# A two-layer hybrid attention block: biases added in PSUM by a two-row product, evictions moved to ScalarE, one minimum taken by a reduction

## The chip, the core and the metric

The kernel runs on one core of one Trainium2 chip. The metric is the device time of one execution in microseconds; of several runs the median counts. TensorE (PE), VectorE (DVE), ScalarE (ACT), GpSimd (POOL) and SyncE (SP) each work through their own queue of instructions in order. Transfers are issued from the queues of SP and ACT.

## What is computed

The reference is a two-layer block over 2048 latent tokens and 256 context tokens of width 1024. Cut to what matters here:

```python
h = rmsnorm(x, norm_g) * (1.0 + scale) + shift          # and the same for ctx
p = split_proj(h @ w_in + b_in)                         # one projection, 18 parts, 4368 columns
ya = diff_attention(...)   # 4 heads x 2 softmax maps, every query over 2304 keys
yb = hgrn2_mixer(...)      # gated linear recurrence, both directions
yc = window_gqa(...)       # windowed attention with sinks
yd = mlstm_mixer(...)      # both directions; output times sigmoid(og)
mixed = concatenate([ya, yb, yc, yd]) * silu(p[18])
x = x + gate * (mixed @ w_out)

def attend(qs, ks, vs):                                 # differential attention
    s = einsum('mbhqd,mbhkd->mbhqk', qs, ks) * scale    # m = 0, 1: the two maps
    p = softmax(s, axis=-1)
    w = p[0] - lam * p[1]
    return einsum('bhqk,bhkv->bhqv', w, vs)
```

The bias `b_in` of the projection, and the shift that each softmax row gets before its exponential, are what the change touches.

## The kernel before

Each of the two layers goes through the same stages. First the rows are normalised and transposed (`hps`, `ht`), and split into two half-precision parts `hh` and `hl`. The weights are scaled by 256 (`WS`) and split the same way by `load_w`. A product of the projection is then three matmuls in 16 bits for each of 8 chunks of the inner dimension.

The projection has two forms. `proj_fm` gives column blocks with the features on the partitions; their bias is a column and comes in with ACT's eviction. `proj_tm` ("token-major") gives 128 tokens on the partitions; here the bias runs along the free dimension. For these `bias_row` loads the bias broadcast over all 128 partitions into a tile `bg` with two buffers, and DVE evicts the PSUM tile `ptm` by one `scalar_tensor_tensor` (`stt`, line 111: times 1/256, plus `bg`). Nine weight blocks of a layer are token-major: VA, MV, HI, SV, OG and four GATE blocks. The tiles that take evictions come from two tags that rotate: `tmp` (six buffers) and `tmp2` (tag `t2`, three buffers).

After the first blocks (VA, KA, QA) runs the loop over differential attention. It has 72 units (a head and 128 queries) in layer 0 and 64 in layer 1. In each unit and for each map `m` (1 first, then 0), `diff_scores` computes the scores in two PSUM tiles, `sc0` of 1024 columns and `sc1` of 1280, one buffer each, and DVE takes the minimum of each (line 1048). The smaller of the two minima is the row's shift (line 1054 for map 1, an operation of the helper `tt` at line 108; line 1056 for map 0). `diff_exp` exponentiates both tiles on ACT. The next map's scores need the PSUM tiles free, that is, after those exponentials. `diff_mix` combines the maps of the unit before on DVE (line 111, `p<-p,sm,p`), ACT rounds the result, and POOL computes the rest of the rounding (`p<-p,p`, line 108).

The other weight blocks of the layer (`other_blocks`) are a "filler": a heavy and a light list of blocks, whose matmuls `pump` lays between those of attention. How much is pumped is fixed in `pe_ns`, an account of TensorE time that `mm` keeps at 2.4 GHz: `FSTEP` between the two score tiles and `FGAP` after each map. A block whose weights were just requested waits `WLOAD` (22,000 to 32,192 ns of that account) before it goes on. In this loop TensorE's order is that of the code; the other engines' order comes from a scheduler, which also brings a transfer forward as soon as its tile has a free buffer. What is left of the filler after the last unit runs in `rest_stream`, beside the start of windowed attention and mLSTM. The last stage of a layer weaves windowed attention, mLSTM, HGRN2 and the output projection (`fx`).

Of the kernel before, what the change touches and what calls it, by code (L numbers as in the profile page):

```python
# [10 lines left out]
F32 = mybir.dt.float32  # L11
# [35 lines left out]
IWS = 1.0 / WS  # L47
GROUPS = [(0, 512), (512, 512), (1024, 512), (1536, 512), (2048, 256)]
# [25 lines left out]
def kernel(  # L74
# [44 lines left out]
    SP.dma_start(ident, masks[:, 0:P])  # L119

# [138 lines left out]
    for l in range(n_layers):  # L259
# [252 lines left out]
        def proj_tm(w, ts, n):  # L512

            yield True
            ps = pps.tile([P, 512], F32, tag="pp", name="ptm")
            for i, t in enumerate(ts):
                g, o = t // 4, (t % 4) * P
                d = ps[:, i * n:(i + 1) * n]
                for k in range(KC):
                    h_, l_ = hh[g][:, k, o:o + P], hl[g][:, k, o:o + P]  # L520
                    mm(d, h_, w[:, 0, k], k == 0, False)
                    mm(d, h_, w[:, 1, k], False, False)
                    mm(d, l_, w[:, 0, k], False, k == KC - 1)
                    yield
            return ps[:, :len(ts) * n].rearrange("p (t c) -> p t c", c=n)
# [68 lines left out]
        def bias_row(c0, n):  # L594

            bg = stg.tile([P, 272], F32, tag="bg", name="bg", bufs=2)[:, :n]
            SP.dma_start(bg, b_in[l, c0:c0 + n].partition_broadcast(P))
            return bg

        def tm_out(w, ts, bg, n):  # L600
            ps = yield from proj_tm(w, ts, n)
            s = tmp2("tm")[:, :len(ts) * n].rearrange("p (t c) -> p t c", c=n)
            stt(s, ps, IWS, bc(bg, 1, len(ts)), ALU.mult, ALU.add)
            return s
# [8 lines left out]
        def proj_store_tm(w, c0, dst, need=True):  # L613
            bg = bias_row(c0, 256)
            for ts in tile_sets(2, need):
                s = yield from tm_out(w, ts, bg, 256)
                DQ.dma_start(rows_of(dst, ts), s)

        def proj_split_tm(w, n, c0, dst):
            nh = n // 64  # L620
            bg = bias_row(c0, n)
            for ts in tile_sets(2):
                s = (yield from tm_out(w, ts, bg, n)).rearrange("p t (h d) -> p t h d", d=64)
                s16 = stg.tile([P, 2, 4, P], F16, tag="sp", name="s16", bufs=2)
                sv = s16[:, :len(ts), :nh]
                A.copy(sv[:, :, :, 0:64], s)
                tt(G, sv[:, :, :, 64:128], s, sv[:, :, :, 0:64], ALU.subtract)
                for i, t in enumerate(ts):
                    DQ.dma_start(dst[t * P:(t + 1) * P], sv[:, i])

        def mix_values(w, gates):

            bg = bias_row(C_MV, 272)
            for t in all_tiles():
                ps = (yield from proj_tm(w, [t], 272))[:, 0]
                s = tmp("tm")
                stt(s[:, :272], ps, IWS, bg, ALU.mult, ALU.add)
                V.tensor_copy(gates[:, t], s[:, 256:272])
                DQ.dma_start(dmv[t * P:(t + 1) * P], s[:, :256])
# [270 lines left out]
        def gate_silu(w, cb):  # L910
            bg = bias_row(C_GATE + cb * 256, 256)
            for ts in tile_sets(2, cq):
                ps = yield from proj_tm(w, ts, 256)
                z, a_ = tmp2("gz"), tmp2("ga")
                stt(z.rearrange("p (t c) -> p t c", c=256), ps, IWS, bc(bg, 1, 2), ALU.mult, ALU.add)
                V.tensor_scalar(z, z, ZLOW, None, ALU.max)
# [31 lines left out]
        def other_blocks():  # L948
# [4 lines left out]
            def values(w):  # L953
# [16 lines left out]
                ((C_OG, 256), lambda w: proj_store_tm(w, C_OG, dog, cq)),  # L970
# [57 lines left out]
        with ExitStack() as st2:  # L1028
# [7 lines left out]
            def diff_scores(u, m):  # L1036
# [16 lines left out]
                if m:  # L1053
                    u["nm"] = tt(V, sm[:, 5:6], sm[:, o:o + 1], sm[:, o2:o2 + 1], ALU.min)
# [146 lines left out]
        with ExitStack() as st4:  # L1201
# [166 lines left out]
            def mlstm_load(i):  # L1368
# [25 lines left out]
                V.tensor_scalar(og, og, ZLOW, None, ALU.max)  # L1394
# [339 lines left out]
```

## Time and profile before

| | us |
|---|---|
| median of 3 runs | 4094.21 |
| lowest and highest | 4089.32 to 4104.06 |
| the profiled execution, whole | 4102.18 |
| its span, first to last instruction | 4100.4 |

The span leaves 1.8 us of the profiled execution outside. That execution is 8.0 us above the median. TensorE's mean granted clock was 0.913 of its full speed. Busy time of an engine is the time in which it had an instruction under way; idle time is put down to what ended it.

### The profile page before, as it was taken

Reading aid. Unit: us, or ns where it says so; the run is one execution under the profiler, and the core shown is the slowest. Engines: PE = TensorE matmul, PEld = TensorE weight load, DVE = VectorE, ACT = ScalarE, POOL = GpSimd, SP = SyncE. Lnnn points to the kernel's source line nnn. Section 1 sums busy time; section 2 is a strip of 40 time slices with the busy share of each in tenths; the row PEclk is TensorE's granted clock in tenths of the full one; section 3 lists DMA queues with packets and bytes.
Section 4 is the critical chain, followed back from the end, with each engine's and each line's share of the span. In section 5 each row is a group of like instructions: output and inputs, shape, how many; then the busy total and the mean of one; then the engine's idle time right before and its main releaser. Section 6 shows DMA issues by size and latency. Waiting matters only on the chain. (4 is left out here: it accounts for less than half of the span.)

```text
span 4100.4 us, 77666 instructions
## 1 busy us (share of the span) xinstructions
PE 3358.2 (82%) x29798; PEld 2269.8 (55%) x29798; DVE 2831.4 (69%) x4343; ACT 2330.9 (57%) x4662; POOL 2375.0 (58%) x1701
## 2 busy tenths in 40 slices
PE   6988878888768996888888988778887698758888
PEld 4656645444546765555557466444445476545554
DVE  5158888888896647465544398988888865467665
ACT  4245655556655636566654266656666665456764
POOL 4443455443445538798966535665334564488885
PEclk8999989999989995898889999999998899869999
DMA  6356866667656628577845457667676584366783
GB/s 211 91 149 150 186 136 159 140 141 154 145 128 157 161 95 200 149 194 185 205 119 177 126 125 151 135 140 155 148 162 142 125 193 116 106 162 170 183 194 104
DMA packets 1267259, 622.12 MB, mean 152 GB/s; under 512 B 931972, under 2 KB 1214152, under 8 KB 1266888
## 3 DMA queue, kind: packets, MB, share of 16 engines
q1 hardware_dynamic: 1164520, 490.65, 53.1%
q10 hardware_dynamic: 102368, 126.52, 9.2%
q8 instruction: 234, 3.83, 0.4%
q14 instruction: 137, 1.12, 0.1%
HBM read 291.76 MB, written 131.23 MB: 103 GB/s over the span
## 5 line engine op out<-in xcount | busy, mean ns | idle before, releaser
L108 POOL TENSOR_TENSOR p<-p,p 128x1024 f16<-128x1024 f32 (+2 forms) x264 | 629.4, 2385 | 792.7 <-ACT p L1084 722.8
L105 ACT ACTIVATE p<-scr,sm 128x1024 f32<-128x1024 f32 (+2 forms) x528 | 628.3, 1194 | 417.8 <-DVE sm L1073 145.2
L94 PE MATMUL ptm<-wb,hh 128*128 128x256 f16 (+2 forms) x5024 | 835.6, 273 | 32.6 <-DVE dSs L111 7.9
L1048 DVE TENSOR_REDUCE sm<-scr 128x1 f32<-128x1024 f32 (+2 forms) x528 | 699.3, 1327 | 218.3 <-PE scr L94 214.5
L94 PE MATMUL pfm<-hh,wb 128*128 128x512 f16 (+1 forms) x2592 | 805.7, 375 | 32.7 <-DVE gz L111 10.1
L94 PE MATMUL ptm<-wb,hl 128*128 128x256 f16 (+2 forms) x2512 | 672.1, 273 | 1.7 <-POOL hl L108 1.7
L94 PEld LDWEIGHTS <-wb 128*128 128x128 f16 x3888 | 378.1, 101 | 414.3 <-issue 84.0
L94 PE MATMUL scr<-Ks,Qs 128*128 128x512 f16 (+1 forms) x1296 | 364.8, 381 | 284.5 <-ACT p L105 279.4
L94 PEld LDWEIGHTS <-hh 128*128 128x128 f16 x5024 | 480.1, 100 | 133.9 <-issue 40.0
L94 PE MATMUL pfm<-hl,wb 128*128 128x512 f16 (+1 forms) x1296 | 485.6, 375 | 0.0
L111 DVE SCALAR_TENSOR_TENSOR p<-p,sm,p 128x1024 f32<-128x1024 f32 (+2 forms) x264 | 413.8, 1568 | 8.1
L94 PEld LDWEIGHTS <-Qs 128*128 128x128 f16 x1296 | 130.7, 102 | 425.2 <-issue 354.5
L94 PE MATMUL fx<-wo,mh 128*128 128x512 f16 x1088 | 342.4, 396 | 16.8 <-DVE xt L111 8.5
L1084 ACT CAST p<-p 128x1024 f16<-128x1024 f32 (+2 forms) x264 | 297.7, 1128 | 39.2 <-DVE p L111 33.8
L94 PEld LDWEIGHTS <-wt 128*128 128x128 f16 x4640 | 243.9, 102 | 71.4 <-DMA wt<-p 24.4
L94 PE MATMUL pv<-Vs,wt 128*128 128x128 f16 (+1 forms) x4640 | 258.5, 213 | 21.9 <-DMA wt<-p 13.5
L94 PEld LDWEIGHTS <-hl 128*128 128x128 f16 x2512 | 250.8, 100 | 35.4 <-POOL hl L108 3.4
L108 POOL TENSOR_TENSOR ph<-swp,ph 128x640 f16<-128x640 f32 (+2 forms) x136 | 196.0, 1442 | 53.7 <-ACT ph L1335 44.3
L108 POOL TENSOR_TENSOR E<-lk,cm 128x512 f32<-128x512 f32 (+1 forms) x136 | 204.8, 1506 | 34.6 <-DMA cm<-dhc 17.8
L94 PE MATMUL fx<-wo,mlo 128*128 128x512 f16 x544 | 212.9, 391 | 1.4 <-DVE mlo L108 1.1
L105 ACT ACTIVATE E<-E 128x1024 f32<-128x1024 f32 x136 | 143.2, 1054 | 102.8 <-POOL E L108 98.9
L108 DVE TENSOR_TENSOR QQ<-hq,E 128x512 f32<-128x512 f32 x119 | 143.8, 1214 | 65.2 <-ACT E L105 46.7
(301 smaller groups left out, 6577.2 us busy)
## 6 DMA issues: line engine op xcount, KB each, us to landing
wraw<-in_w_in_dram SPq DMA_DIRECT2D x60, 512.0 KB
dgt<-ga ACTq DMA_DIRECT2D x68, 256.0 KB
r1b<-dr SPq DMA_DIRECT2D x68, 256.0 KB
gtt<-dgt SPq DMA_DIRECT2D x34, 512.0 KB
mraw<-in_w_mod_dram SPq DMA_DIRECT2D x64, 256.0 KB
vi<-dhi SPq DMA_DIRECT2D x49, 256.0 KB
KSb<-dsk SPq DMA_DIRECT2D x56, 192.0 KB
Ks<-dka SPq DMA_DIRECT2D x64, 144.0 KB
```

What stands on the lines that cost most here:

```text
L94: PE.matmul(o, lhsT=lhsT, rhs=rhs, start=start, stop=stop)
L105: A.activation(out=o, in_=i, func=f, **kw)
L108: return e.tensor_tensor(out=o, in0=a, in1=b, op=op)
L111: V.scalar_tensor_tensor(out=o, in0=a, scalar=s, in1=b, op0=op0, op1=op1)
L1048: V.tensor_reduce(sm[:, m * 2 + j:m * 2 + j + 1], ps[:, :n], AX.X, ALU.min)
L1084: A.copy(wl[:, :n], p[:, :n])
```

## The change

A constant tile `bones` of 2 x 128 elements, all 16.0, is made once. `bias_row` now loads the bias to two partitions only, into a buffer of the tag `t2`, and makes from it a two-row half-precision tile by five small DVE instructions: scale, round, subtract, mask, combine. Row 0 is the rounded bias, row 1 the rest. In `proj_tm` each tile's accumulation in PSUM begins with a product of `bones` with these two rows, so that the bias is in PSUM. The evictions of HI and MV become ACT copies, the two halves of VA and SV come straight from PSUM (ACT the rounded one, DVE the rest, where POOL computed it before), and the evictions of OG and GATE become one DVE `tensor_scalar` that also applies the floor `ZLOW`. The two instructions that applied that floor before (lines 916 and 1394) are gone. Map 1's shift is taken by one `tensor_reduce` over the two minima, in place of a `tensor_tensor` of the two.

```diff
@@ -45,6 +45,7 @@
 EPS = 1e-6
 WS = 256.0
 IWS = 1.0 / WS
+BONES = 16.0
 GROUPS = [(0, 512), (512, 512), (1024, 512), (1536, 512), (2048, 256)]
 C_QA, C_KA, C_VA = 0, 256, 512
 C_HQ, C_FF, C_FB, C_HI = 768, 1024, 1280, 1536
@@ -117,6 +118,8 @@
     V.memset(eps_t, EPS)
     V.memset(one_t, 1.0)
     SP.dma_start(ident, masks[:, 0:P])
+    bones = const.tile([2, P], F16, tag="bones", name="bones")
+    V.memset(bones, BONES)
 
     def rstd_of(o, ss, n):
 
@@ -509,16 +512,17 @@
                 yield
             return ps
 
-        def proj_tm(w, ts, n):
+        def proj_tm(w, ts, n, bg):
 
             yield True
             ps = pps.tile([P, 512], F32, tag="pp", name="ptm")
             for i, t in enumerate(ts):
                 g, o = t // 4, (t % 4) * P
                 d = ps[:, i * n:(i + 1) * n]
+                mm(d, bones, bg, True, False)
                 for k in range(KC):
                     h_, l_ = hh[g][:, k, o:o + P], hl[g][:, k, o:o + P]
-                    mm(d, h_, w[:, 0, k], k == 0, False)
+                    mm(d, h_, w[:, 0, k], False, False)
                     mm(d, h_, w[:, 1, k], False, False)
                     mm(d, l_, w[:, 0, k], False, k == KC - 1)
                     yield
@@ -593,14 +597,23 @@
 
         def bias_row(c0, n):
 
-            bg = stg.tile([P, 272], F32, tag="bg", name="bg", bufs=2)[:, :n]
-            SP.dma_start(bg, b_in[l, c0:c0 + n].partition_broadcast(P))
+            bf = tmp2("bg")[0:2, :n]
+            SP.dma_start(bf, b_in[l, c0:c0 + n].partition_broadcast(2))
+            hv, bg = [stg.tile([2, 272], F16, tag=f"bg{j}", name="bg16", bufs=1 + j)[:, :n] for j in range(2)]
+            V.tensor_scalar(bf, bf, WS / BONES, None, ALU.mult)
+            V.tensor_copy(hv, bf)
+            tt(V, bf, bf, hv, ALU.subtract)
+            V.tensor_scalar(bf, bf, ident[0:2, 1:2], None, ALU.mult)
+            stt(bg, hv, ident[0:2, 0:1], bf, ALU.mult, ALU.add)
             return bg
 
-        def tm_out(w, ts, bg, n):
-            ps = yield from proj_tm(w, ts, n)
+        def tm_out(w, ts, bg, n, low=False):
+            ps = yield from proj_tm(w, ts, n, bg)
             s = tmp2("tm")[:, :len(ts) * n].rearrange("p (t c) -> p t c", c=n)
-            stt(s, ps, IWS, bc(bg, 1, len(ts)), ALU.mult, ALU.add)
+            if low:
+                V.tensor_scalar(s, ps, IWS, ZLOW, ALU.mult, ALU.max)
+            else:
+                act(s, ps, AF.Copy, scale=IWS)
             return s
 
         def tile_sets(per, need=True):
@@ -610,21 +623,22 @@
         def rows_of(dst, ts):
             return dst[ts[0] * P:(ts[0] + len(ts)) * P].rearrange("(t p) ... -> p t ...", p=P)
 
-        def proj_store_tm(w, c0, dst, need=True):
+        def proj_store_tm(w, c0, dst, need=True, low=False):
             bg = bias_row(c0, 256)
             for ts in tile_sets(2, need):
-                s = yield from tm_out(w, ts, bg, 256)
+                s = yield from tm_out(w, ts, bg, 256, low)
                 DQ.dma_start(rows_of(dst, ts), s)
 
         def proj_split_tm(w, n, c0, dst):
             nh = n // 64
             bg = bias_row(c0, n)
             for ts in tile_sets(2):
-                s = (yield from tm_out(w, ts, bg, n)).rearrange("p t (h d) -> p t h d", d=64)
-                s16 = stg.tile([P, 2, 4, P], F16, tag="sp", name="s16", bufs=2)
-                sv = s16[:, :len(ts), :nh]
-                A.copy(sv[:, :, :, 0:64], s)
-                tt(G, sv[:, :, :, 64:128], s, sv[:, :, :, 0:64], ALU.subtract)
+                s = (yield from proj_tm(w, ts, n, bg)).rearrange("p t (h d) -> p (t h) d", d=64)
+                s16 = stg.tile([P, 2, 512], F16, tag="sp", name="s16", bufs=2).rearrange("p a (h d) -> p (a h) d", d=P)
+                s16 = s16[:, :len(ts) * nh]
+                act(s16[:, :, 0:64], s, AF.Copy, scale=IWS)
+                stt(s16[:, :, 64:128], s, IWS, s16[:, :, 0:64], ALU.mult, ALU.subtract)
+                sv = s16.rearrange("p (t h) d -> p t h d", h=nh)
                 for i, t in enumerate(ts):
                     DQ.dma_start(dst[t * P:(t + 1) * P], sv[:, i])
 
@@ -632,10 +646,10 @@
 
             bg = bias_row(C_MV, 272)
             for t in all_tiles():
-                ps = (yield from proj_tm(w, [t], 272))[:, 0]
+                ps = (yield from proj_tm(w, [t], 272, bg))[:, 0]
                 s = tmp("tm")
-                stt(s[:, :272], ps, IWS, bg, ALU.mult, ALU.add)
-                V.tensor_copy(gates[:, t], s[:, 256:272])
+                act(s[:, :256], ps[:, 0:256], AF.Copy, scale=IWS)
+                act(gates[:, t], ps[:, 256:272], AF.Copy, scale=IWS)
                 DQ.dma_start(dmv[t * P:(t + 1) * P], s[:, :256])
 
         carry = stg.tile([P, 2, 65], F32, tag="carry", name=f"carry{l}")
@@ -910,10 +924,9 @@
         def gate_silu(w, cb):
             bg = bias_row(C_GATE + cb * 256, 256)
             for ts in tile_sets(2, cq):
-                ps = yield from proj_tm(w, ts, 256)
+                ps = yield from proj_tm(w, ts, 256, bg)
                 z, a_ = tmp2("gz"), tmp2("ga")
-                stt(z.rearrange("p (t c) -> p t c", c=256), ps, IWS, bc(bg, 1, 2), ALU.mult, ALU.add)
-                V.tensor_scalar(z, z, ZLOW, None, ALU.max)
+                V.tensor_scalar(z.rearrange("p (t c) -> p t c", c=256), ps, IWS, ZLOW, ALU.mult, ALU.max)
                 sigmoid(a_, z)
                 tt(G, a_, a_, z, ALU.mult)
                 DQ.dma_start(rows_of(dgt, ts)[:, :, cb * 256:(cb + 1) * 256], a_.rearrange("p (t c) -> p t c", c=256))
@@ -967,7 +980,7 @@
             light = [
                 ((C_HI, 256), lambda w: proj_store_tm(w, C_HI, dhi)),
                 ((C_SV, 128), lambda w: proj_split_tm(w, 128, C_SV, dsv)),
-                ((C_OG, 256), lambda w: proj_store_tm(w, C_OG, dog, cq)),
+                ((C_OG, 256), lambda w: proj_store_tm(w, C_OG, dog, cq, True)),
                 ((C_MQ, 256), lambda w: proj_store_fm(w, 13, 1.0, dmq, cq)),
                 ((C_HQ, 256), lambda w: proj_store_fm(w, 7, 0.125, dhq, cq)),
             ] + [((C_GATE + cb * 256, 256), lambda w, cb=cb: gate_silu(w, cb)) for cb in range(4)]
@@ -1051,7 +1064,7 @@
                 o2 = o + len(hs) - 1
 
                 if m:
-                    u["nm"] = tt(V, sm[:, 5:6], sm[:, o:o + 1], sm[:, o2:o2 + 1], ALU.min)
+                    u["nm"] = V.tensor_reduce(sm[:, 5:6], sm[:, o:o2 + 1], AX.X, ALU.min)
                 else:
                     u["nm"] = V.tensor_scalar(sm[:, 4:5], sm[:, o:o + 1], sm[:, o2:o2 + 1], shf, ALU.min, ALU.add)
 
@@ -1391,7 +1404,6 @@
                     tt(G, r1b[:, d], r1b[:, d], bc(mlm[:, d], 1, 4), ALU.add)
                     for h in range(4):
                         act(r1b[:, d, h], r1b[:, d, h], AF.Exp, bias=TM[:, 0, d, js[d] * 4 + h:js[d] * 4 + h + 1])
-                V.tensor_scalar(og, og, ZLOW, None, ALU.max)
                 sigmoid(og, og)
                 return js, qt_, kt_, v1, r1b, g0b, og
 
```

## Rows read from the trace of the kernel before

**Rows 1.** Windows: length, busy us of PE, PEld, DVE, ACT, POOL, clock, DMA, GB/s.
```profile
300.00:1350.00 1050.00, 850.03 (x7440) 569.11 (x7433) 855.78 (x1277) 616.36 (x1054) 487.24 (x297) 0.93 0.67 150
1350.00:1450.00 100.00, 92.74 (x809) 70.78 (x808) 60.12 (x116) 55.04 (x125) 52.67 (x47) 0.98 0.59 149
1450.00:1580.00 130.00, 112.07 (x974) 84.26 (x972) 70.06 (x120) 60.59 (x116) 67.59 (x57) 0.85 0.46 128
1580.00:2115.00 535.00, 439.23 (x4598) 306.44 (x4601) 313.56 (x549) 336.24 (x895) 460.11 (x363) 0.84 0.72 179
...
2370.00:3255.00 885.00, 703.46 (x6217) 460.75 (x6215) 786.64 (x1099) 560.94 (x874) 433.73 (x236) 0.94 0.67 144
```

**Rows 2.** Waits in layer 0's attention loop, 300 to 1350 us.
```profile
PE scr L94 <- ACT p L105: 117.2, 81, 7.1
```

**Rows 3.** Waits in layer 1's attention loop, 2400 to 3330 us.
```profile
PE scr L94 <- ACT p L105: 141.8, 103, 6.3
```

**Rows 4.** Instructions on tile sm (ns min/median/max, first and last start).
```profile
L108 DVE TENSOR_TENSOR sm<-sm x136: 127/772/2330, 247.9 to 3240.4; 128x1 f32<-128x1 f32 x136
L1056 DVE TENSOR_SCALAR sm<-sm,shf x136: 244/272/277, 257.2 to 3248.0; 128x1 f32<-128x1 f32 x136
L1073 DVE TENSOR_REDUCE sm<-sm x136: 136/144/158, 263.0 to 3252.4; 128x2 f32<-128x4 f32 x128, 128x2 f32<-128x2 f32 x8
```

**Rows 5.** Timeline of one unit, 2808 to 2814 us (start, us, instruction, idle before).
```profile
2808.90 2.61 POOL L108 TENSOR_TENSOR p<-p,p 128x1280 f16<-128x1280 f32 x1 [3.35 <-ACT p L1084]
...
2810.41 1.12 DVE L108 TENSOR_TENSOR sm<-sm 128x1 f32<-128x1 f32 x1
...
2811.62 1.11 ACT L105 ACTIVATE p<-scr,sm 128x1024 f32<-128x1024 f32 x1 [1.65 <-DVE sm L1073]
...
2812.20 1.28 DVE L111 SCALAR_TENSOR_TENSOR p<-p,sm,p 128x1024 f32<-128x1024 f32 x1
...
2812.88 0.59 PE L94 MATMUL scr<-Ks,Qs 128*128 128x512 f16 x2 [0.67 <-ACT p L105]
...
2813.51 1.23 DVE L1048 TENSOR_REDUCE sm<-scr 128x1 f32<-128x1024 f32 x1
```

**Rows 6.** Groups by line and shape (busy us, mean ns, idle before).
```profile
L108 DVE TENSOR_TENSOR sm<-sm 128x1 f32<-128x1 f32 x136 | 97.8, 719 | 0.6
...
L916 DVE TENSOR_SCALAR gz<-gz 128x512 f32<-128x512 f32 x68 | 47.4, 697 | 1.4
...
L722 ACT COPY kT<-ktp 128x512 f32<-128x512 f32 x32 | 18.5, 578 | 20.8 <-PE ktp L101 14.5 <-POOL ga L108 3.6 <-DVE gz L111 2.4
...
L111 DVE SCALAR_TENSOR_TENSOR tm<-ptm,bg 128x272 f32<-128x272 f32 x36 | 15.6, 432 | 2.0 <-PE ptm L94 2.0
L638 DVE COPY gates<-tm 128x16 f32<-128x16 f32 x36 | 15.2, 421 | 0.2
...
L163 ACT COPY mrow<-modps 128x256 f32<-128x256 f32 x32 | 11.9, 372 | 14.5 <-PE modps L94 14.4
```

**Rows 7.** Instructions on tile gz, whole run.
```profile
L111 DVE SCALAR_TENSOR_TENSOR gz<-ptm,bg x68: 659/683/693, 1067.4 to 3568.0; 128x512 f32<-128x512 f32 x68
L916 DVE TENSOR_SCALAR gz<-gz x68: 395/460/2197, 1069.2 to 3569.1; 128x512 f32<-128x512 f32 x68
```

**Rows 8.** The last of the 136 pairs, minimum and scores behind it (timeline).
```profile
3240.41 0.15 DVE L108 TENSOR_TENSOR sm<-sm 128x1 f32<-128x1 f32 x1
...
3241.84 1.01 PE L94 MATMUL scr<-Ks,Qs 128*128 128x512 f16 x2 [4.45 <-ACT p L105]
```

**Rows 9.** Timeline of block VA: three token-major products in a row.
```profile
111.04 0.38 PE L94 MATMUL ptm<-wb,hh 128*128 128x256 f16 x2
...
111.37 0.38 PE L94 MATMUL ptm<-wb,hh 128*128 128x256 f16 x2
```

**Rows 10.** Timeline: a bias row's transfer, and the first eviction that uses it.
```profile
495.02 0.53 SPq L597 DMA_DIRECT2D bg<-in_b_in_dram  x1
...
1067.45 0.68 DVE L111 SCALAR_TENSOR_TENSOR gz<-ptm,bg 128x512 f32<-128x512 f32 x1
```

## The prediction

> **What bounds the kernel now.** I read first the busy times by stretch. No stretch is idle and no engine is the bound of all of them. The two loops over attention take 1050 and 885 us, nearly half of the span; there DVE is busy for 82% and 89%, TensorE for 81% and 79% [rows 1]. Behind the first loop, where the rest of the filler runs, TensorE is busy for 93% and then 86%: it sets the pace. In the last stage of layer 0 POOL is busy for 460 of 535 us [rows 1].
>
> Next the waits inside the loops. TensorE's wait before a score tile, ended by ACT's exponential, sums to 117 us in layer 0 and 142 us in layer 1, together 259 us [rows 2, 3]. That is most of TensorE's idle time there (200 and 182 us by [rows 1]). So a cycle sets the pace of the loop: scores, the two minima on DVE, the smaller of them, exponential on ACT, next scores. The filler is laid into it by an account and fills the gaps only partly. Whoever shortens the cycle shortens the loop, until the 259 us are used up.
>
> Then the small instruction that takes the smaller minimum. Map 1's is a `tensor_tensor` of one element per partition; it takes 127 ns at least, 772 ns at the median and 2330 ns at most. Its neighbours of the same size hardly vary: 244 to 277 ns for map 0's `tensor_scalar`, 136 to 158 ns for a two-element `tensor_reduce` [rows 4]. The timeline of one unit says why: POOL's subtraction runs from 2808.90 to 2811.51, the minimum begins at 2810.41 and ends at 2811.53, with POOL [rows 5]. I compared all 136 minima with POOL's instructions, the first at 247.9 and the last at 3240.4 [rows 4]: of the 83 that took over 0.2 us, 82 end within 0.06 us of the end of a POOL instruction. DVE waits for POOL inside the instruction. The exponential, and then the next scores, wait behind it.
>
> **The change part by part.**
>
> *Map 1's minimum.* Removed: 136 times 719 ns, 97.8 us [rows 6]. Added: 136 reductions of two elements, 0.146 us each by the nearest row [rows 4]: 20 us. DVE gets back 78 us. What of it reaches the end of the loop depends on whether TensorE waited behind that minimum. I took each minimum and the wait of the scores behind it; the last pair is 0.15 us and 4.45 us [rows 8]. Summing the smaller of "duration less 0.14" and "wait" over the 136 pairs gives 57 us. A second limit is DVE's own order: after the minimum come three small instructions and the mix of the two maps (`p<-p,sm,p`), and the next minimum of scores follows directly, at 2813.51 after 2812.20 plus 1.28 [rows 5]. The mix has two tensor inputs too and may still wait for POOL. Then only the 0.67 us from the end of the minimum (2811.53) to the mix (2812.20), which now pass while POOL works, and about 0.1 us of the minimum itself are won. With a cap of 0.75 us per unit the sum over the pairs is 45 us. I take 48; bounds 15 (a third of the capped sum) and 57.
>
> *DVE's other relief in the loop.* HI's 18 evictions at 0.683 us [rows 7] are 12 us, MV's 36 evictions and 36 copies of gates are 15.6 and 15.2 us [rows 6], all moved to ACT. The 68 floors of GATE at 0.697 us are 47 us [rows 6]; by their starts 25 of them (the first at 1069.2 [rows 7]) fall into the loops, some 17 us. Together about 60 us of DVE time in a cycle in which DVE is busy for 82 to 89%. The minimum's own relief, 78 us, gave 45 to 57 us by the pairs, over half; here instructions stand anywhere in the cycle, so I take a third: 22 us, bounds 8 and 35. OG's and GATE's evictions stay on DVE at about the 0.68 us that they take. VA and SV keep one instruction each on DVE and on ACT, and POOL is freed of 36 subtractions, which I count as nothing: POOL is busy for less than half of the loops.
>
> *Outside the loops.* Some 40 floors of GATE and 34 of OG go, the latter on half as many columns, together some 50 us of DVE time, where TensorE or POOL sets the pace [rows 1]. I take 5 us, bounds 0 and 15.
>
> *ACT's new evictions.* HI: 18 at 0.578 us, by the PSUM copy of the same shape; MV: 36 at 0.372 and 36 of 16 columns at about 0.2 (an estimate, by the two fixed parts of those two rows: 0.578 less twice the 0.206 for 256 columns leaves 0.17) [rows 6]. That is 10 + 13 + 7 = 30 us on an engine that is busy for 59 to 63% of the loops and belongs to the cycle. I take a sixth on the path: 5 us, bounds 0 and 20.
>
> *The two-row products.* There are 162 tiles in layer 0 and 152 in layer 1 (five blocks leave out the two context tiles), 314 products. A row of two partitions is not in the trace; nearest are products of 256 columns over all rows: from 111.04 to 111.37 three begin, 0.11 us each [rows 9]. I price the new ones alike, since what streams is the same columns; SV's 36 have half. That is 278 x 0.11 + 36 x 0.055 = 33 us at full clock. In the loops the filler is metered by the account, which counts these products, so each unit takes the same TensorE time and the surplus moves behind the loop, where TensorE sets the pace. I take nine tenths of it as lost: 30 us, bounds 25 and 36 (33 divided by the mean clock of 0.913).
>
> *The bias rows.* 18 blocks, five DVE instructions each on up to 272 columns: 90. Nearest are 0.16 us at least (it must exceed a two-element reduction's 0.146 [rows 4]) and the 0.46 us median of the floor on 512 columns [rows 7]. Seven blocks get their bias inside the loops; 35 instructions at 0.33 are 12 us of DVE, of which I count 5 on the path, bounds 3 and 20. The floor's maximum of 2197 ns beside its median of 460 shows that this kind of instruction can be held up as the minimum was [rows 7]. The Trainium skill ("SBUF — State Buffer", "SBUF: two separate sides") says that GpSimd and VectorE share a port pair which the first one holds for a whole instruction, against VectorE instructions with two SBUF inputs or in a two-port mode; 82 of the 83 slow minima agree. By that rule most of the five can be held up like the floor, at its mean of 0.697 us: 63 us of DVE in all instead of 30, and 9 or 10 us on the path instead of 5. I stay with 5, because they can run long before they are needed; the upper bound covers the rest.
>
> *The wait for the bias.* It was needed at a block's first eviction and is now needed at its first product, with all of TensorE's queue behind it, in the loop the next unit's scores too. Before, the transfer ran up to 572 us ahead (495.02, first used at 1067.45 [rows 10]). Now it needs one of the three buffers of `t2`, which the evictions of the block before rotate through. But a block waits 22 to 32 us for its weights, so those are done by then. I count nothing; the rival below has the price.
>
> **Sum.** -48 - 22 - 5 + 5 + 30 + 5 = -35 us. The profiled execution took 4102.2, its span 4100.4 with 1.8 us around it, so it would take 4067. It lay 8 us above the median of the runs shown; the prediction of the median is 4094 - 35, rounded to 4060.
>
> **The rivals.**
>
> *More is won.* Pairs without the cap (57), the other relief in full (35), 15 outside, and small costs (0 + 25 + 3): -79, 4015. For it speaks that 259 us of waits are there to be used up [rows 2, 3]; against it that DVE stays close to full.
>
> *The wait moves on.* The minimum no longer waits for POOL, but the mix behind it does, and the next minimum of scores is behind the mix on DVE. If the reach is a third (15), other relief 8, nothing outside, costs as above (+40): +17, 4111. The rule of the skill named above would have it so, for the mix has two SBUF inputs. Against it: what stands between, 0.67 us, runs under POOL's time, and ACT starts earlier in any case [rows 5].
>
> *Slower: blocks wait for their bias.* Place: the first product of each of 18 blocks. Price: a transfer, then five dependent instructions in DVE's queue between those of a unit that fills DVE for over 80%. At 5 us a block it is 90 us, 4150; from 35 / 18 = 1.9 us a block on the gain is gone. For it speaks that the tile comes from a busy tag; against it the long lead of the transfer before [rows 10].
>
> **How the numbers follow.** Forecast (4035 to 4080) 0.55; more won 0.18; the wait moves on 0.13; blocks wait 0.10; something else, such as an unlucky order by the scheduler, 0.04. Under 0.3%, 12 us, a measurement of this kernel can't tell a difference from none (its three runs span 15 us). Faster: 0.55 + 0.18 and a little of the others, 0.75. Of the wait that moves on about half lies within 12 us, with part of the others: 0.11 the same, 0.14 slower. The range takes in more won (with 10 us below it) and ends at the wait that moves on: 4005 to 4112; beyond lies the slower rival.
>
> **What would show it.** Right: map 1's new reduction takes about 0.15 us with no spread, and the waits of scores for the exponential fall well below 259 us while both loops end earlier, together by some 65 us. The loops' gain should be partly given back behind them, about 15 us a layer. The mix's mean time on DVE may rise. Wrong: first products of a block that wait for DVE's bias tile; loops as long as before, with the same waits named after the mix or after ACT's evictions; or two-row products that take much more than 0.11 us.

## The result: 1.5% slower, and the profile after

| | median of runs (us) | lowest to highest | profiled run, its span | mean granted clock |
|---|---|---|---|---|
| before | 4094.26 (4) | 4089.32 to 4104.06 | 4102.2, 4100.4 | 0.913 |
| changed | 4155.61 (4) | 4139.32 to 4171.28 | 4171.28, 4169.2 | 0.910 |

The ratio of the medians is 1.015, its 95% interval 1.010 to 1.019. The forecast was 4060 in 4005 to 4112: the changed kernel lies 44 us above the upper end, on the other side of the kernel before. The profiled run of the changed kernel is the slowest of its four, 16 us above their median, so its stages add up to 69 us more than before and not to 61.

I divide both spans into stages at events of their timelines. "Start" ends with the first feature-major product (`pfm`), 92 us of preparation follow, a loop runs from its first score product to its last value product, "rest" is what follows up to the last token-major product, and "end" is the remainder of the layer (layer 1 begins with its first product `hps`; the last 3 us of the span, behind the last transfer's issue, are left out). Three of the experiments below stand beside the two kernels; layer 1's short start and preparation are one row. All are lengths in us of one profiled run.

| stage | before | changed | minimum alone (r1) | no bias at all (r4) | products uncounted (r9) |
|---|---|---|---|---|---|
| start 0 | 145.1 | 164.8 | 144.2 | 145.2 | 163.7 |
| preparation 0 | 92.5 | 91.0 | 92.7 | 89.7 | 93.5 |
| loop 0 | 1034.8 | 1027.6 | 1013.5 | 1009.9 | 1022.6 |
| rest 0 | 267.3 | 303.4 | 264.6 | 264.6 | 275.4 |
| end 0 | 626.0 | 641.4 | 621.1 | 621.0 | 611.7 |
| start and preparation 1 | 164.3 | 174.9 | 162.0 | 162.9 | 176.0 |
| loop 1 | 949.8 | 926.6 | 914.5 | 920.8 | 930.0 |
| rest 1 | 285.5 | 314.2 | 287.3 | 285.8 | 298.0 |
| end 1 | 531.7 | 521.9 | 520.6 | 522.7 | 520.1 |

Both loops of the changed kernel are shorter, by 7 and 23 us. Behind them 36 and 29 us are lost, the start of layer 0 loses 20 and that of layer 1 11. The end stages differ by up to 30 us from kernel to kernel without a pattern that I could tie to an edit. The changed kernel's 641.4 us in end 0 are such a case: r2 below, which differs from it by the minimum alone, takes 28 us less there. Gains and losses of single stages, of one run each, are to be read with that in mind.

The minimum became what was forecast. Instructions on tile sm of the changed kernel, as [rows 4]:

```profile
L1067 DVE TENSOR_REDUCE sm<-sm x136: 133/146/156, 266.7 to 3291.4; 128x1 f32<-128x2 f32 x128, 128x1 f32<-128x1 f32 x8
```

The long tail is gone: 156 ns at most, where the `tensor_tensor` took up to 2330. The wait of the scores for the exponential between 300 and 1350 us, 117.2 us before [rows 2], is now:

```profile
PE scr L95 <- ACT p L106: 85.5, 58, 6.1
```

What the two-row product does to TensorE stands in block VA's timeline. The PE rows are start, us, instruction; the weight load's row (PEld) has its idle time before it:

```profile
117.75 0.27 PE L95 MATMUL ptm<-wb,hl 128*128 128x256 f16 x1
117.96 0.28 PE L95 MATMUL ptm<-bg,bones 2*128 2x256 f16 x1
118.17 0.39 PE L95 MATMUL ptm<-wb,hh 128*128 128x256 f16 x2
```

```profile
117.95 0.09 PEld L95 LDWEIGHTS <-bones 2*128 2x128 f16 x1 [0.21 <-issue]
```

From the last product of one tile (117.75) to the first of the next (118.17), 0.42 us pass with one product between. Products over all rows start 0.11 us apart [rows 9], so one of them would make it 0.22. The two-row product costs 0.31 instead of 0.11: its weight load begins only at 117.95, with 0.21 us of idle time before it, and the product behind it starts as late again.

And the bias is late at the start. Timeline, 68 to 110 us:

```profile
68.33 0.43 SPq L601 DMA_DIRECT2D bg<-in_b_in_dram  x1
...
104.71 0.81 DVE L423 TENSOR_SCALAR ht<-hps,modA,md 128x512 f32<-128x512 f32 x1 [0.30 <-POOL hl L109]
...
105.61 2.55 DVE L603 TENSOR_SCALAR bg<-bg 2x256 f32<-2x256 f32 x1
...
109.33 0.47 DVE L112 SCALAR_TENSOR_TENSOR bg<-bg,ident,bg 2x256 f16<-2x256 f16 x1
...
109.85 0.37 PE L95 MATMUL ptm<-bg,bones 2*128 2x256 f16 x1 [8.07 <-DVE bg L112]
```

The transfer is issued at 68.33. The first of the five DVE instructions begins 37 us later, behind the `ht` of the norm stage in DVE's queue. The first token-major product stands behind it at 109.85. In the kernel before it came at 49.38:

```profile
49.38 0.63 PE L94 MATMUL ptm<-wb,hh 128*128 128x256 f16 x2
```

From 45 to 110 us the kernel before runs 114 token-major products of this block between the norm's own; the changed kernel runs one, the last row above. TensorE is busy there for 32 us where it was for 45 (windows as in [rows 1], before and then changed):

```profile
45.00:110.00 65.00, 45.03 (x264) 31.30 (x261) 49.48 (x62) 42.91 (x85) 51.71 (x46) 0.82 0.36 135
```

```profile
45.00:110.00 65.00, 32.06 (x151) 22.88 (x147) 51.96 (x67) 41.57 (x83) 49.93 (x44) 0.77 0.34 129
```

These products have to be done afterwards, and layer 0's start is 19.7 us longer.

### The profile page after: what moved, and what is told of

Same layout as the page of the kernel before. It is cut to its first block, busy times and chain, and to the rows that moved or that the text cites. A ratio compares the mean times of both kernels' runs of the same rounds, so it can differ in the third digit from the quotient of the medians.

```text
span 4169.2 us, 78201 instructions
## 1 busy us (share of the span) xinstructions
PE 3449.2 (83%) x30112; PEld 2277.9 (55%) x30112; DVE 2735.7 (66%) x4242; ACT 2349.9 (56%) x4752; POOL 2339.1 (56%) x1665
## 5 line engine op out<-in xcount | busy, mean ns | idle before, releaser
L95 PE MATMUL ptm<-wb,hh 128*128 128x256 f16 (+2 forms) x5024 | 850.4, 274 | 0.0
L95 PEld LDWEIGHTS <-hh 128*128 128x128 f16 x5024 | 458.5, 100 | 141.7 <-issue 39.7
L112 DVE SCALAR_TENSOR_TENSOR p<-p,sm,p 128x1024 f32<-128x1024 f32 (+2 forms) x264 | 427.8, 1621 | 9.7 <-POOL p L109 0.5
L109 DVE TENSOR_TENSOR QQ<-hq,E 128x512 f32<-128x512 f32 x119 | 157.6, 1331 | 73.8 <-ACT E L106 42.2
```

What stands on the lines that cost most here:

```text
L95: PE.matmul(o, lhsT=lhsT, rhs=rhs, start=start, stop=stop)
L109: return e.tensor_tensor(out=o, in0=a, in1=b, op=op)
L112: V.scalar_tensor_tensor(out=o, in0=a, scalar=s, in1=b, op0=op0, op1=op1)
```

## The experiments

Ratios are to the kernel before, run beside each of them on the same chip (its medians there: 4093 to 4098 us). All intervals are 95%. A difference of two kernels below is therefore good to some 12 us, and to some 20 where the changed kernel is one of the two. r4, r5, r6 and r8 leave the bias out of the result; they serve for the time alone.

| kernel | median us | ratio | interval |
|---|---|---|---|
| r1: minimum alone | 4027.0 | 0.983 | 0.981 to 0.985 |
| r2: changed, old minimum | 4193.4 | 1.025 | 1.022 to 1.028 |
| r3: changed, product over 128 rows | 4155.4 | 1.014 | 1.011 to 1.017 |
| r4: changed, no bias at all | 4020.2 | 0.981 | 0.978 to 0.983 |
| r5: changed, two rows, constant zero | 4119.4 | 1.006 | 1.004 to 1.008 |
| r6: changed, 128 rows, constant zero | 4094.6 | 1.000 | 0.998 to 1.002 |
| r7: rows ready, product over 36 rows | 4122.5 | 1.007 | 1.005 to 1.010 |
| r10: rows ready, product over 128 rows | 4101.9 | 1.001 | 0.999 to 1.003 |
| r8: rows made, no products | 4029.8 | 0.984 | 0.982 to 0.986 |
| r11: r10, products uncounted | 4056.5 | 0.990 | 0.988 to 0.993 |
| r9: changed, products uncounted | 4096.8 | 1.000 | 0.998 to 1.001 |
| r12: r1, and `dn` with one operand from PSUM | 4032.9 | 0.985 | 0.983 to 0.987 |

**The minimum by itself (r1), and the rest by itself (r2).** r1 is the kernel before with one line of the change:

```diff
-                    u["nm"] = tt(V, sm[:, 5:6], sm[:, o:o + 1], sm[:, o2:o2 + 1], ALU.min)
+                    u["nm"] = V.tensor_reduce(sm[:, 5:6], sm[:, o:o2 + 1], AX.X, ALU.min)
```

> The kernel before with one edit: map 1's shift by the tensor_reduce; biases as before. Theory A (the minimum's gain is there, the two-row products ate it): the two loops over attention end earlier by 45 to 57 us together, the whole takes 4040 to 4055. Theory B (the wait for POOL only moves to the mix behind it): 4085 to 4105, and the mix's mean on DVE rises from 1568 ns by about what the minimum lost.

r2 is the changed kernel with that line taken back.

> The changed kernel with map 1's shift taken by the tensor_tensor as before. Theory A: the minimum's gain is lost on top, 4195 to 4215. Theory B: within 10 us of the changed kernel, 4145 to 4165.

r1 took 4027.0, 71 us less than the kernel before beside it and below the 4040 to 4055 of theory A. It is faster than both kernels. Its instructions on tile sm and its two loops in the windows (length, busy us of PE, PEld, DVE, ACT, POOL, clock, DMA, GB/s):

```profile
L1054 DVE TENSOR_REDUCE sm<-sm x136: 123/145/156, 247.4 to 3173.1; 128x1 f32<-128x2 f32 x128, 128x1 f32<-128x1 f32 x8
```

```profile
236.90:1250.40 1013.50, 824.95 (x7275) 546.36 (x7274) 837.58 (x1264) 607.86 (x999) 479.60 (x269) 0.94 0.69 152
...
2298.20:3212.70 914.50, 741.89 (x6531) 487.67 (x6530) 793.74 (x1154) 591.14 (x916) 467.99 (x255) 0.94 0.69 147
```

The loops are 21 and 35 us shorter than before, 56 together, which is what theory A said of them, and nothing is given back behind them (264.6 and 287.3 us, before 267.3 and 285.5). Of the rest of the gain, 16 us in the profiled runs lie in the end stages, where this edit changes nothing. The mix behind the minimum hardly takes over the wait. Groups by shape, before and then in r1:

```profile
L111 DVE SCALAR_TENSOR_TENSOR p<-p,sm,p 128x1280 f32<-128x1280 f32 x128 | 235.1, 1837 | 0.0
...
L111 DVE SCALAR_TENSOR_TENSOR p<-p,sm,p 128x1024 f32<-128x1024 f32 x128 | 172.3, 1346 | 7.6
```

```profile
L111 DVE SCALAR_TENSOR_TENSOR p<-p,sm,p 128x1280 f32<-128x1280 f32 x128 | 233.9, 1827 | 0.0
...
L111 DVE SCALAR_TENSOR_TENSOR p<-p,sm,p 128x1024 f32<-128x1024 f32 x128 | 187.1, 1462 | 7.6
```

The second form is 116 ns slower now, 15 us of DVE time over 128 of them, against the 78 us that the minimum sets free.

r2 took 4193.4, next to theory A's range: without the minimum the other edits cost 95 us. In the changed kernel the minimum is worth 38 us, not 71. In the profiled runs the missing part is loop 0: it takes 1027.6 us in r2 and 1027.6 in the changed kernel, while loop 1 takes 957.4 and 926.6.

**Is it the row change of TensorE, or the bias? (r3, r4).** My first reading was that the 0.31 us explain the loss: 314 times 0.2 us more than priced is 63 us. r3 keeps everything, with stationary and bias tile on 128 partitions that are zero but for two:

```diff
-    bones = const.tile([2, P], F16, tag="bones", name="bones")
-    V.memset(bones, BONES)
+    bones = const.tile([P, P], F16, tag="bones", name="bones")
+    V.memset(bones, 0.0)
+    V.memset(bones[0:2], BONES)
...
-            hv, bg = [stg.tile([2, 272], F16, tag=f"bg{j}", name="bg16", bufs=1 + j)[:, :n] for j in range(2)]
+            hv = stg.tile([2, 272], F16, tag="bg0", name="bg16", bufs=1)[:, :n]
+            bgz.append(bgz.pop(0))
+            bg = bgz[0][0:2, :n]
...
-            return bg
+            return bgz[0][:, :n]
```

> The changed kernel, with the constant and the bias tile on all 128 partitions, zero but for the two rows, so that the bias product has the same rows as its neighbours; the result is the same. Theory A (TensorE loads the weights of the two-row product, and those behind it, only when the product before has ended: 0.32 us each in place of 0.11): 314 x 0.21 = 66 us less, 4080 to 4100. Rival C (the loss is in the bias rows' preparation, the waits for them and ACT's evictions): 4140 to 4165, with the products' spacing unchanged or of no consequence.

r4 leaves products and bias rows out and keeps the new evictions and the minimum:

```diff
-                mm(d, bones, bg, True, False)
...
-                    mm(d, h_, w[:, 0, k], False, False)
+                    mm(d, h_, w[:, 0, k], k == 0, False)
```

> The changed kernel without the two-row products and without the bias rows (the token-major parts go without their bias); evictions and minimum stay changed. Theory A: 314 x 0.32 = 100 us and the late starts of the two VA blocks (20 and 10 us) go: 4020 to 4045. Rival C, with products at 0.11 us: 33 us and the starts, 4085 to 4100. If ACT's evictions are the loss, 4110 or more.

r3's products now start like any other. Timeline of its block VA:

```profile
117.67 0.27 PE L95 MATMUL ptm<-wb,hl 128*128 128x256 f16 x1
117.78 0.27 PE L95 MATMUL ptm<-bgz,bones 128*128 128x256 f16 x1
117.89 0.38 PE L95 MATMUL ptm<-wb,hh 128*128 128x256 f16 x2
```

0.11 us each, and yet 4155.4, the same as the changed kernel. So the first reading falls, and with it theory A. r4 took 4020.2: the bias's way into PSUM costs 135 us. That is the edge of theory A's range for r4, but with r3 beside it the row change can't be the whole of it. r4 and r1 differ by 7 us with overlapping intervals: the evictions on ACT and the dropped floors are together worth nothing that these runs can tell; no run takes the two apart.

**The products without the rows (r5, r6).** Both feed the product with a constant zero that is ready from the start, r5 over two rows and r6 over 128. They take away the 18 transfers and 90 instructions of the bias rows, and with them every wait for a bias. r5's edit, without the lines that it removes from `bias_row` (in r6 `bz` and `bones` have 128 rows):

```diff
+    bz = const.tile([2, 272], F16, tag="bz", name="bz")
+    V.memset(bz, 0.0)
...
-            return bg
+            return bz[:, :n]
```

> The changed kernel with the 314 two-row products kept, but on a constant row of zeros: no bias transfers, no DVE instructions for them, nothing to wait for (the token-major parts go without their bias). Against the run without products and rows (4020): Theory A' (the products' own TensorE time at 0.31 us each is most of the loss): 4100 to 4125. Theory D (the products cost 0.11 us each and the rest is waiting for late bias rows): 4045 to 4065.

> As the run before it, with the constant on all 128 partitions, so that each product takes 0.11 us. Both theories have 34 us over 4020 here: 4045 to 4065. The difference to the two-row form is the price of the change of rows alone: 60 us by A', under 15 by D. If it is near 4150, neither holds and it is what the products do to the account and the order.

r5 came out in the range of theory A' (4119.4), but r6, at 4094.6, lies 30 us above what both theories had said for it. r6 against r4: 314 ordinary products and nothing else cost 74 us. r5 against r6: two rows in place of 128 cost 25 us. The changed kernel against r5: making the rows and getting them late costs 36 us.

**The rows ready early, with the bias itself (r7, r10).** All 18 rows are made once, with 18 transfers and 8 DVE instructions near the start, on the partitions 2b and 2b + 1 of block b; the stationary selects them. r7's product runs over these 36 rows, r10's over 128. r7's edit, without the lines that make the rows:

```diff
-                mm(d, bones, bg, True, False)
+                mm(d, bg[0], bg[1], True, False)
...
-            return bg
+            b_ = l * 9 + BLK.index(c0)
+            return bsel[0:36, b_:b_ + 1].broadcast_to([36, P]), ball[0:36, :n]
```

> The changed kernel with all 18 bias rows made together near the start (eight DVE instructions in all) and kept; each block picks its two rows by a product over 36 rows. The result is the same. Theory D: no block waits for its bias; the two VA blocks start as before (20 and 10 us back): 4050 to 4085. Theory A': the products still change the rows, 4100 to 4130.

> As the run before it, the product over all 128 rows. Both theories: neither a change of rows nor a late bias is left, only 314 x 0.11 us: 4045 to 4070, slower than the kernel before with the reduction alone (4027). If it stays above 4100, the loss is in what the products displace.

They come out near r5 and r6 (4122.5 and 4101.9), r7 where theory A' had it, r10 above both theories, on the side that its text ties to what the products displace: 36 rows cost 20 us over 128. So with early rows the row change costs 20 to 25 us, and a bias that is ready in time saves some 33 us of the changed kernel (4155.6 to 4122.5).

**The rows without the products (r8).** r4 with the bias rows made as in the changed kernel and used by nobody.

> The changed kernel with its bias rows loaded and made as they are (90 small DVE instructions), but without the products that use them (the token-major parts go without their bias). Against the run without both (4020) it prices the instructions alone: if they load DVE's chain, 4040 to 4060; if only the waiting of TensorE for them costs, within 12 us of it, 4010 to 4032.

4029.8, 10 us above r4 with intervals that overlap: inside the 12 us that the text allows for instructions of little weight. The rows' own instructions are the smaller part of the 36 us; the rest is that TensorE needs them.

**Why do 33 us of products cost 74? (r11, r9).** The loops lay filler in by an account of TensorE's time, and each new product of 256 columns is charged 107 ns there (its columns at 2.4 GHz). Then the loop holds fewer tiles of projection, and these come where TensorE sets the pace. Both kernels take the products out of the account, r11 in r10 and r9 in the changed kernel itself. r9's edit:

```diff
+                t0 = pe_ns[0]
                 mm(d, bones, bg, True, False)
+                pe_ns[0] = t0
```

> The run with ready bias rows and full-row products (4102), the products left out of the account that meters the filler; the result is the same. If their dearness (75 us for 34 us of TensorE time) comes from what they displace behind the loops: the stretches behind the loops get back some 15 us each, the loops give up less than that, 4070 to 4090. If TensorE's time in the loops is as dear as behind them: 4095 to 4110.

> The changed kernel itself (two rows, bias rows made late), its products left out of the account; the result is the same. If the parts found so far add up (4020, 36 for late rows, 25 for the change of rows, 75 for counted or 30 for uncounted products): 4155 - 45 = 4100 to 4120, still not faster than the kernel before by much, if at all. If the account only mattered without the waits, 4135 to 4160.

r11 is 45 us faster than r10, at 4056.5 beyond the 4070 to 4090 that was expected. r9 is 59 us faster than the changed kernel, where 35 to 55 were expected: 4096.8, which can't be told from the kernel before. The windows of loop 0 and of the stretch behind it, first the changed kernel, then r9:

```profile
255.90:1283.50 1027.60, 856.16 (x7284) 550.18 (x7283) 807.05 (x1220) 616.22 (x1037) 464.85 (x259) 0.92 0.68 148
1283.50:1586.90 303.40, 276.07 (x2240) 196.85 (x2238) 128.92 (x257) 139.08 (x300) 128.60 (x119) 0.96 0.45 124
```

```profile
257.20:1279.80 1022.60, 851.97 (x7382) 549.36 (x7381) 820.26 (x1228) 619.80 (x1045) 471.50 (x260) 0.94 0.68 150
1279.80:1555.20 275.40, 259.69 (x2103) 185.27 (x2101) 116.50 (x238) 134.27 (x290) 125.09 (x117) 0.98 0.50 132
```

r9's loop holds 98 matmuls more and is not longer, but 5 us shorter. The stretch behind it holds 137 fewer and is 28 us shorter: 16 us of busy time and 12 of idle. The groups of TensorE in that stretch say what was moved (busy us, mean ns, idle before), again the changed kernel and then r9:

```profile
L95 PE MATMUL ptm<-wb,hh 128*128 128x256 f16 x865 | 149.1, 277 | 0.0
...
L95 PE MATMUL ptm<-bg,bones 2*128 2x256 f16 x54 | 15.3, 283 | 9.6 <-DVE bg L112 6.6 <-ACT fm L106 2.1 <-DVE gz L929 1.0
```

```profile
L95 PE MATMUL ptm<-wb,hh 128*128 128x256 f16 x810 | 137.9, 275 | 0.0
...
L95 PE MATMUL ptm<-bg,bones 2*128 2x256 f16 x50 | 13.9, 279 | 4.4 <-ACT fm L106 2.5 <-DVE dSs L112 1.4 <-DVE gz L931 0.4
```

865 products with `hh` against 810 are three to four tiles of projection that went back into the loop, and 810 stand there in the kernel before as well. The loop didn't get longer by them. They are some 85 of the 137 matmuls, 9 us at 0.11 us each; most of the others belong to HGRN2 (`dS`, 240 and 208; `ktp`, 60 and 52) and moved into the end stage, because the stretch ends sooner. Part of the 12 us idle is one wait for a bias row, 6.57 us in the changed kernel, which fell into its stretch behind the loop and has no counterpart in r9. So the stretch is 28 us shorter for 9 us of projection; that it is more than the projection's own length is measured, the whole of the reason is not. Of the 75 us between these two profiled runs another 30 lie in end 0, which I can't tie to the edit.

**Another instruction of the same kind (r12).** r1's gain raises the question whether more is to be had from small instructions that wait for POOL. In r1, 45 of the 46 instructions on `dn` that took over 0.25 us end 16 to 25 ns after a POOL instruction. The mLSTM's `dn` is made by a `tensor_tensor` of two small tiles in the last stage; r12 is r1 with `dn` taken straight from PSUM, so that only one operand comes from SBUF:

```diff
-                        act(dn, nv[:, :, 64], AF.Abs)
-                        tt(V, dn, dn, TM[:, 2, d, js[d] * 4:js[d] * 4 + 4], ALU.max)
+                        stt(dn, nv[:, :, 64], -1.0, TM[:, 2, d, js[d] * 4:js[d] * 4 + 4], ALU.mult, ALU.max)
+                        stt(dn, nv[:, :, 64], 1.0, dn, ALU.mult, ALU.max)
```

> The kernel before with the reduction (4027), and in mLSTM the maximum of 4 elements per partition rewritten: ACT's absolute value and DVE's tensor_tensor of two SBUF operands become two scalar_tensor_tensor with one operand in PSUM, of the same result. If a DVE instruction with one SBUF operand is not held up by POOL, the two take about 0.2 us each without spread, in place of 144 to 1450 ns, and the end stages gain 5 to 25 us: 4002 to 4022. If it is the size of the instruction or its place that makes it wait, their spread stays and the time is 4020 to 4034.

Instructions on tile dn, in r1 and then in r12 (ns min/median/max):

```profile
L108 DVE TENSOR_TENSOR dn<-dn,TM x68: 144/534/1450, 1282.8 to 3972.4; 128x4 f32<-128x4 f32 x68
```

```profile
L111 DVE SCALAR_TENSOR_TENSOR dn<-mnum,TM x68: 131/150/164, 1285.3 to 3981.1; 128x4 f32<-128x4 f32 x68
L111 DVE SCALAR_TENSOR_TENSOR dn<-mnum,dn x68: 137/161/164, 1285.5 to 3981.3; 128x4 f32<-128x4 f32 x68
```

The hold-up is gone, 1450 ns at most becoming 164, but the gain of 5 to 25 us that was expected of it did not come: the time is 4032.9, not below r1's 4027.0. This one was not on the path.

## Why the prediction was wrong

**Map 1's minimum: right, with its size too small.** DVE was held by POOL inside the instruction, the reduction is not, and the loops shrink. I took 48 us, with 57 as the upper bound; alone it gave 71. Of these the two loops hold 56 in the profiled runs, what the sum over the pairs had said without the cap (57). The cap of 0.75 us per unit rested on the mix taking over the wait, and in r1 its two forms took over 15 us of 78. In the changed kernel the minimum was worth 38.

A reading of the trace was off as well: 300 to 1350 and 2370 to 3255 us are not the loops, which by their first score product and last value product run from 237.6 to 1272.4 and from 2330.0 to 3279.8. The waits for the exponential sum to 279 us in them, not 259, and to 242 in r1: most of them are still there after the gain, so they were no measure of what could be won. Only 18 of GATE's 68 floors lie in these loops, not 25. The sum over the pairs doesn't rest on the windows.

**DVE's other relief and ACT's evictions: nothing to be seen.** I had -22, -5 and +5. r4 holds these edits with the minimum and is 7 us below r1, within the error, and its two loops take 1931 us together where r1's take 1928. So the relief of DVE, less what ACT's new work costs, bought next to nothing in the loops; a relief that ACT's work eats up again is not excluded. That a third of any DVE time in the loop comes back as time of the loop is not borne out; the minimum, which stands between scores and exponential, gave most of its 78 us.

**The two-row products: the step that failed.** It reads "I price the new ones alike" and, of the surplus, "30 us, bounds 25 and 36". The runs give 74 us for products over all rows (r6 less r4) and 25 for the two rows (r5 less r6). That is 99 us where I took 30. Two things were missed. The first is the row change itself: 0.42 us from full row to full row in place of 0.22. The second is the account. I counted that the surplus moves behind the loop, at its own length. But the loop has idle TensorE time in which the products are nearly free (r9's loop 0 holds 98 matmuls more and is 5 us shorter), and the account displaced tiles of projection for them, which behind the loop cost more than their length: of the 28 us in rest 0 that r9 gains, 16 are busy time and 12 idle. That the account is the cause is shown by r9 and r11, which change nothing else: 59 and 45 us. It is not the whole: r11 still stands 36 us above r4, which has neither products nor rows. That is near the 30 that I had taken: the price would fit products over all rows that the account doesn't count, and the two-row products were counted.

**The bias rows: 5 us forecast, 10 measured (r8 less r4), which the intervals hardly tell from none.** The 90 instructions take 58 us of DVE in the changed kernel, not the 30 that I priced; the 63 that I worked out for instructions held up like the floor was nearer.

**The wait for the bias: the second step that failed, "I count nothing".** The rival "blocks wait for their bias" had the right mechanism and too high a price. TensorE's waits for the bias (sum in us, how many, the longest), and the two longest behind the 8.07 of the start, in the timeline:

```profile
PE ptm L95 <- DVE bg L112: 19.5, 4, 8.1
```

```profile
1518.50 0.27 SPq L601 DMA_DIRECT2D bg<-in_b_in_dram  x1
...
1525.92 1.13 DVE L603 TENSOR_SCALAR bg<-bg 2x256 f32<-2x256 f32 x1
...
1529.71 0.39 PE L95 MATMUL ptm<-bg,bones 2*128 2x256 f16 x1 [6.57 <-DVE bg L112]
...
3339.37 0.28 PE L95 MATMUL ptm<-bg,bones 2*128 2x256 f16 x1 [4.39 <-DVE bg L112]
```

I asked how long before its use the transfer ran. At the start it still runs 41 us ahead (68.33 to 109.85). I did not ask what the five instructions behind it queue after on DVE: in block VA all of the norm's `ht`. Behind loop 0 the lead itself is gone: the transfer is issued 11 us before the first product that needs it; DVE begins on the row 7 us after the issue and takes 4 to make it. In the kernel before, the same block's transfer was issued at 1349.47 and first used at 1483.79. "So those are done by then" failed here: SyncE waited 3.4 us, up to 1518.46, for the landing of a store from the block before, which reads a tile of the tag `t2`. The prediction named "the first product of each of 18 blocks" for the wait; only four have one that shows, the longest at the start of layer 0 and two in the stretches behind the loops. The price is 36 us (changed less r5, good to some 20), of which about 10 are the rows' own instructions (r8 less r4).

**The sum.** From r4: 4020 + 74 for counted products + 25 for two rows + 36 for late rows = 4155, the changed kernel's 4155.6. It must add up, for each part is the difference of two neighbours in one chain (r4, r6, r5, changed), and the parts depend on the order in which they are taken: with late rows, two rows or 128 make no difference that the runs can tell (r3, 4155.4), and then late rows cost 61 (r3 less r6). The likely reason is that where TensorE waits for something else the row change hides; no run shows it, so it stays open. Open too is why the minimum is worth 71 us in one kernel and 38 in the other, with no gain in the latter's loop 0.

The range was too narrow because it allowed 36 us at most for the products (they cost 99) and put the wait for the bias at either 0 or 90 (it cost 36). By the prediction's own other terms, -48 - 22 - 5 + 5, these two sizes make +65, and the changed kernel is 61 us slower. That these other terms, -70 in sum, lie near the -78 of r4 is luck: the minimum gave 23 us more than I took and the rest 15 less.

## What to carry to other kernels

Look for small DVE instructions whose median is several times their minimum, ask whether they end with POOL and whether a later queue waits behind them; a form with one SBUF operand (here a reduction) can then give back most of the hold-up (71 us for 78 of DVE time here, nothing for `dn`), and it was all of this change's gain that the runs can tell. Adding a bias in PSUM moves its deadline from the last product of a tile to the first and puts the work on TensorE, so ask first whether the eviction that did it was on any path: here it was not, and the 135 us had nothing to pay for them. Where filler work is metered by an account, an addition that is charged displaces other work, and one that fits into idle time should not be charged.

## What the runs showed of the hardware that I had not expected

A product over two partitions between products over 128 takes 0.31 us of TensorE's queue instead of 0.11, and r7's over 36 partitions takes the same 0.31. The Trainium skill says that a change of tiling mode, and not of the tile alone, drains TensorE ("TensorEngine Tiling (Array Packing)", "Key Properties"); the timeline of r3, where the same product over 128 rows is back at 0.11, would fit that. That the product over few rows runs in another tiling mode is not shown by any run here.

Small one-input instructions from SBUF to SBUF can be held up as well. The bias rows' scaling and cast on two partitions in the changed kernel:

```profile
L603 DVE TENSOR_SCALAR bg<-bg x18: 207/280/2546, 105.6 to 3551.7; 2x256 f32<-2x256 f32 x14, 2x272 f32<-2x272 f32 x2, 2x128 f32<-2x128 f32 x2
L604 DVE CAST bg<-bg x18: 207/282/2380, 108.2 to 3554.2; 2x256 f16<-2x256 f32 x14, 2x272 f16<-2x272 f32 x2, 2x128 f16<-2x128 f32 x2
```

Of these 36, 23 take up to 283 ns; the other 13 take 511 to 2546, and all 13 end 78 to 154 ns after a POOL instruction. The reduction of the minima stays at 156 or less, though 90 of its 136 run beside a POOL instruction. The Trainium skill ("SBUF — State Buffer", "SBUF: two separate sides") names DVE instructions with two SBUF inputs or in a two-port mode as those that can wait for POOL. r12, whose instructions with one operand from PSUM stay at 164 ns or less, agrees with the first half; which mode the scaling and the cast run in no trace here shows.
